# Second and fourth sums of the FFN up-projection weights formed by VectorE adds instead of accumulating DMAs; the first column group in the same order as the others

## The chip, the core and the metric

One NeuronCore of a Trainium2 chip runs the whole program. The metric is device microseconds from the program's start to its end, the median of several executions. The engines have a queue each and work them off in order: TensorE (PE, with its weight loads shown as PEld), VectorE (DVE), ScalarE (ACT), GpSimd (POOL) and SyncE (SP). Here SP issues the plain loads, and POOL issues the loads that add what they bring to what is already in the tile (accumulating DMAs).

## The reference

Two layers of a hybrid decoder trunk on 512 tokens of 1024 features, all float32. Each layer is a mixer with four branches, which the change does not touch, and a feed-forward network (FFN), which it does:

```python
    hf = rmsnorm(x, norm_ffn)
    gate, up = jnp.split(hf @ ffn_w_up, 2, axis=-1)
    return x + (jax.nn.silu(gate) * up) @ ffn_w_down
```

`ffn_w_up` is 1024 x 5632: the first 2816 columns are the gate's, the last 2816 the up half.

## The kernel before

Every float32 operand is split into a high and a low part, and a product is three matmuls (`mm3`): high by high, high by low, low by high. ScalarE makes the high part of a block of weights (`w_hi`), VectorE subtracts it from the raw block for the low part (`w_lo`).

The up-projection is done by the seven products of Strassen's scheme in Winograd's form instead of eight. The columns are taken in six groups (q from 0 to 5) of 512 of the gate's and 512 of the up half's; the last group has 256 of each. The rows (features) are parted into even and odd blocks of 128 and the tokens into two halves. With G0, G1 for the gate's even and odd rows of a group and U0, U1 for the up half's, the products read these blocks of weights (1 MB each):

- p1 reads G0 (in the code `B11` for q = 0), and writes the PSUM pair A
- p5 reads X = G0 + U0, the first sum, and writes C
- p6 reads X + U1, the second sum, and writes B
- p3 reads Y = U1, added to C
- p2 reads G1, added to A
- p7 reads Y + U0, the third sum, added to B
- p4 reads X + U1 + G1, the fourth sum, added to B

(The signs are in the features' sums, the tiles `s_hi` and `s_lo`, which are formed at the end of the mixer, and in the negative of the norm's factor, `nrstd_t`.) Each product is two parts, one per half of its block's rows (h0, h1, 512 KB each), and each part is 12 matmuls on 512 columns. Between products VectorE adds the PSUM pairs to scratch tiles (their names in the profile are `merged`), ScalarE and VectorE form silu times up, PE transposes the result (`turn`), and after groups 2 and 5 the down-projection follows (`down`).

All four sums of weights are formed before by accumulating DMAs: `Block.add` (line 1114) has POOL issue two DMAs with `accum_op=OP.add`. p5 issues those of the second sum at its end, p6 those of the fourth, p3 those of the third, and `first_sum` those of the first. The raw tile w_raw has two buffers, used in turn, and the tile f_raw, which belongs to the FFN alone, two more: X of groups 1 to 5 lies in f_raw, as does p2's block in group 0; all else lies in w_raw. Split blocks have three buffers, so a split can run at most three parts ahead of PE.

The first group has an order of its own, p1, p5, p2, p3, p6, p5 of the next group, p7, p4. All others run p1, p6, p3, p2, p7, p5 of the next group, p4. The order on each engine is set by the scheduler of the framework from the program's order and priorities; splits and additions of PSUM pairs are issued with a high priority. What it makes of the change is shown further down.

Of the kernel before, what the change touches and what calls it, by code (L numbers as in the profile page):

```python
# [17 lines left out]
OP = mybir.AluOpType  # L18
# [5 lines left out]
NT = S // P  # L24
# [19 lines left out]
AHEAD = 3000  # L44
# [25 lines left out]
def hybrid_trunk(ctx: ExitStack, tc: tile.TileContext, x, mem, positions, norm_mix, w_in, conv_w,  # L70
# [155 lines left out]
    def small(n, name="small", bufs=12):  # L226
        return consts.tile([P, 8], F32, name=name, bufs=bufs)[:, :n]
# [94 lines left out]
    def norm_token(ssq):  # L322
        ps = tr_ps()
        for t in range(NT):
            pe.matmul(ps[:, t:t + 1], ssq[:, t * P:(t + 1) * P], ones_d[:, 0:1], start=True, stop=True)
        r = small(NT, name="rstd_t", bufs=2)
        rstd_into(r, ps[:, :NT], small, NT)
        return r
# [772 lines left out]
    class Block:  # L1101
# [12 lines left out]
        def add(self, src, odd):  # L1114
            for i in range(2):
                nc.gpsimd.dma_start(self.raw[:, 2 * i:2 * i + 2, :], self.rows(src, odd, i), accum_op=OP.add)  # L1116
            return self

        def split(self):
            parts = []  # L1120
            for i in range(2):
                hi, lo = (wpool.tile([P, 1024], F32R, name=nm, bufs=W_BUFS)[:, :2 * self.n].rearrange("p (k n) -> p k n", n=self.n)
                          for nm in ("w_hi", "w_lo"))
                with tc.high_priority(offset=AHEAD):
                    A(hi, self.raw[:, 2 * i:2 * i + 2, :], AF.Copy)
                    dve.tensor_sub(lo, self.raw[:, 2 * i:2 * i + 2, :], f(hi))  # L1126
                parts.append((hi, lo))
            return parts

    def ffn(l, h, sx, ssq, xr, spare):  # L1130
# [9 lines left out]
        with tc.tile_pool(name="ffn", bufs=1) as fp:  # L1140
# [3 lines left out]
            def block(n, name="w_raw"):  # L1144
                if name == "w_raw":
                    t = wpool.tile([P, 2048], F32, name="w_raw", bufs=RAW_BUFS)
                else:
                    t = fp.tile([P, 2048], F32, name=name, bufs=2)
                return Block(t[:, :4 * n].rearrange("p (k n) -> p k n", n=n), n)

            def gate_w(q):
                return up[:, q * 512:q * 512 + widths[q]]

            def up_w(q):
                return up[:, FF + q * 512:FF + q * 512 + widths[q]]

            def product(pss, form, parts, first, mid=None):
                src, odd, s0 = form
                n = parts[0][0].shape[2]
                for i, (hi, lo) in enumerate(parts):  # L1160
                    for t in range(2):
                        for k in range(2):
                            kk = 2 * i + k
                            c = kk if odd is None else 2 * kk + odd
                            mm3(pss[t][:, :n], pair(src, c, slice(s0 + t * P, s0 + (t + 1) * P)),
                                (hi[:, k, :], lo[:, k, :]), first and kk == 0, kk == 3, not first)
                    if i == 0 and mid is not None:
                        mid()
# [16 lines left out]
            def accs(name):  # L1185
                return [bank[name]() for _ in range(2)]
# [10 lines left out]
            def p5(q):  # L1197
                d = st[q]
                d["C"] = accs("C")
                product(d["C"], S1, d["X"].split(), True)  # L1200
                d["X"].add(up_w(q), 1)

            def p1(q, mid=None):
                d = st[q]
                d["A"] = accs("A")
                w = d["B11"] if q == 0 else block(widths[q]).load(gate_w(q), 0)
                product(d["A"], A11, w.split(), True, mid)

            def silu_mul(dst, src, t, other):
                A(dst, src, AF.Silu, scale=norm["r"][:, t:t + 1])  # L1210
# [9 lines left out]
            def hi_prio():  # L1220
                return tc.high_priority(offset=AHEAD)
# [13 lines left out]
                residual(lambda m: xr[:, m, :], wd, a, kt, 256, h2, ssq2, lambda c: g_mix(l + 1, c), spill=end)  # L1235
                return h2, ssq2

            def p2(q):
                product(st[q]["A"], A12, block(widths[q], "w_raw" if q else "f_raw").load(gate_w(q), 1).split(), False)

            def p3(q):
                d = st[q]
                d["Y"] = block(widths[q]).load(up_w(q), 1)
                product(d["C"], S4, d["Y"].split(), False)
                d["Y"].add(up_w(q), 0)

            def p4(q):
                product(st[q]["B"], A22, st[q]["X"].split(), False)

            def p6(q):  # L1250
                d = st[q]
                d["B"] = accs("B")
                product(d["B"], S2, d["X"].split(), True)
                d["X"].add(gate_w(q), 1)

            def p7(q):
                product(st[q]["B"], S3, st[q]["Y"].split(), False)

            def plus(dst, src, ps, n):
                with hi_prio():  # L1260
                    for t in range(2):
                        dve.tensor_add(dst[t], src[t], ps[t][:, :n])

            def ahead(q):
                if q < Q:
                    p5(q)

            first_sum(0)
            for q in range(Q):
                n = widths[q]  # L1270
                d1, e, u, g = (tmps(i, n) for i in range(4))
                p1(q, flush)
                d = st[q]
                if q == 0:
                    p5(0)
                with hi_prio():
                    for t in range(2):
                        A(d1[t], d["A"][t][:, :n], AF.Copy)
                plus(e, d1, d["C"], n)
                if q == 0:  # L1280
                    r = norm_token(ssq)
                    nr = small(NT, name="nrstd_t", bufs=2)
                    dve.tensor_scalar(nr, r, -1.0, None, op0=OP.mult)
                    norm.update(r=r, n=nr)
                    p2(q)
                    p3(q)
                    plus(u, d1, d["C"], n)
                    first_sum(q + 1)
                    p6(q)
                    plus(u, u, d["B"], n)  # L1290
                else:
                    p6(q)
                    plus(u, d1, d["B"], n)
                    p3(q)
                    if q + 1 < Q:
                        first_sum(q + 1)
                    plus(u, u, d["C"], n)
                    p2(q)
                for t in range(2):
                    silu_mul(g[t], d["A"][t][:, :n], t, u[t])  # L1300
                if q == 0:
                    p5(q + 1)
                    turn(g, 0, q)
                p7(q)
                plus(e, e, d["B"], n)
                if q:
                    turn(g, 0, q)
                    ahead(q + 1)
                p4(q)
                plus(d1, d1, d["B"], n)  # L1310
                for t in range(2):
                    silu_mul(d1[t], d1[t], t + 2, e[t])
                pending.append((d1, 2, q))
                if q in ends:
                    flush()
                    res = down(q)
# [40 lines left out]
```

## Time and profile before

| what | value |
|---|---|
| timed runs, median of 3 | 2050.01 us (2049.25 to 2051.16) |
| profiled execution, its own time | 2053.13 us |
| its span | 2051.4 us |
| mean granted clock of TensorE | 0.99 |
| FFN of layer 0, of layer 1 (first matmul of p1) | from 712.1 us, from 1697.9 us |
| moved by DMA | 250.01 MB, of which 46.28 MB by POOL's accumulating DMAs and its few others |

The profile's page gives busy time by engine, then the span in 40 slices, the queues, the chain of work that ended last, and the costliest groups. In its rows "L284 PE MATMUL B<-w_hi,s_hi" is line, engine, operation and the tiles it writes and reads; a bracket at the end holds the idle time of the engine just before the instruction and what ended it. Matmuls overlap, so the time between the starts of two of them is their cost. Times in the timeline are us from the span's start. "SPq" and "POOLq" are DMAs issued by SP and POOL, with the time from issue to landing.

### The profile page before, as it was taken

The numbers are of one execution on the slowest core, as the hardware profiler recorded it, in microseconds if no ns is written. First come the engines' busy times: TensorE is split into PE (matmuls) and PEld (weight loads), VectorE is DVE, ScalarE is ACT, GpSimd is POOL, SyncE is SP. The second block draws the span as 40 slices with busy tenths as digits, with TensorE's granted clock in tenths as the row PEclk, the third lists the DMA queues.
The fourth block names the chain that finished last, engine by engine and source line by source line (L and its number), as shares of the span: only waits on it lengthen the run. The fifth ranks groups of instructions, "written<-read, shape, count | busy, mean of one in ns | idle before, by whom it ended". The sixth has DMA issues, their size and how long they took to land.

```text
span 2051.4 us, 27620 instructions
## 1 busy us (share of the span) xinstructions
PE 2014.5 (98%) x10440; PEld 1699.4 (83%) x10440; DVE 1374.4 (67%) x2673; ACT 1112.9 (54%) x1978; POOL 126.5 (6%) x132
## 2 busy tenths in 40 slices
PE   7899999999999989999999999999999999999999
PEld 7898988888888868888889898878888887888887
DVE  5668899637766757537656899963677676663662
ACT  6554565866565535324445555577667655541541
POOL 1000000000000022102100000000000002210210
PEclk8999999999999999999999999999999999999999
DMA  6622122212214498738452222221222349782852
GB/s 219 231 94 88 57 93 93 93 62 83 83 62 151 120 222 194 176 113 185 104 184 74 93 77 93 93 93 42 82 74 81 128 119 228 188 209 99 174 128 92
DMA packets 190904, 250.01 MB, mean 122 GB/s; under 512 B 6690, under 2 KB 134772, under 8 KB 190644
## 3 DMA queue, kind: packets, MB, share of 16 engines
q1 hardware_dynamic: 160800, 193.55, 28.8%
q0 software_dynamic: 26368, 46.28, 13.3%
q10 hardware_dynamic: 3604, 8.43, 1.1%
q8 instruction: 82, 1.34, 0.3%
q14 instruction: 50, 0.41, 0.1%
HBM read 237.74 MB, written 10.49 MB: 121 GB/s over the span
## 4 chain that ended last, share of the span: by engine, by line
PE 90%; DMA 5%; issue 2%; DVE 1%; POOL 1%; ACT 1%; SPq 0%; POOLq 0%; ACTq 0%
PE mm L284 18%; PE mm L285 18%; PE mm L286 18%; PE B L284 4%; PE B L286 4%; PE B L285 4%; PE A L286 3%; PE A L285 3%; PE A L284 3%; DMA w_raw<-in_ffn_w_up_dram 2%; DMA f_raw<-in_ffn_w_up_dram 1%; PE C L285 1%; PE C L284 1%; PE C L286 1%; PE tr L734 1%
## 5 line engine op out<-in xcount | busy, mean ns | idle before, releaser
L119 ACT ACTIVATE w_hi<-w_raw 128x1024 fp32r<-128x1024 f32 (+1 forms) x362 | 373.2, 1032 | 440.6 <-PE mm L285 137.3
L249 DVE TENSOR_TENSOR w_lo<-w_raw,w_hi 128x1024 fp32r<-128x1024 f32 x258 | 311.9, 1210 | 223.0 <-ACT w_hi L119 219.6
L284 PE MATMUL mm<-h_hi,w_hi 128*128 128x512 f32 x960 | 378.7, 395 | 0.0
L285 PE MATMUL mm<-h_lo,w_hi 128*128 128x512 f32 x960 | 377.3, 393 | 0.0
L286 PE MATMUL mm<-h_hi,w_lo 128*128 128x512 f32 x960 | 375.3, 393 | 0.0
L286 PEld LDWEIGHTS mm<-h_hi,w_lo 128*128 128x128 f32 x960 | 180.4, 188 | 37.5 <-issue 0.7
L284 PEld LDWEIGHTS mm<-h_hi,w_hi 128*128 128x128 f32 x960 | 180.5, 188 | 37.3 <-issue 2.0
L285 PEld LDWEIGHTS mm<-h_lo,w_hi 128*128 128x128 f32 x960 | 180.5, 188 | 36.7 <-issue 1.7
L1126 DVE TENSOR_TENSOR w_lo<-w_raw,w_hi 128x1024 fp32r<-128x1024 f32 (+1 forms) x104 | 118.8, 1142 | 94.4 <-ACT w_hi L119 93.8
L286 PE MATMUL mm<-w_hi,h_lo 128*128 128x256 f32 (+1 forms) x448 | 127.9, 286 | 0.0
L284 PE MATMUL mm<-w_hi,h_hi 128*128 128x256 f32 (+1 forms) x448 | 127.1, 285 | 0.0
L285 PE MATMUL mm<-w_lo,h_hi 128*128 128x256 f32 (+1 forms) x448 | 126.9, 284 | 0.0
L284 PE MATMUL mm<-y_hi,w_hi 128*128 128x512 f32 x256 | 102.3, 401 | 0.0
L286 PE MATMUL mm<-y_hi,w_lo 128*128 128x512 f32 x256 | 101.5, 397 | 0.0
L285 PE MATMUL mm<-y_lo,w_hi 128*128 128x512 f32 x256 | 101.3, 396 | 0.0
L1116 POOL DMA_DIRECT2D f_raw<-in_ffn_w_up_dram x60 | 75.5, 1287 | 414.9 <-DVE w_lo L1126 337.7
L1126 DVE TENSOR_TENSOR w_lo<-f_raw,w_hi 128x1024 fp32r<-128x1024 f32 (+1 forms) x64 | 72.0, 1125 | 39.7 <-ACT w_hi L119 39.4
L119 ACT ACTIVATE w_hi<-f_raw 128x1024 fp32r<-128x1024 f32 (+1 forms) x64 | 62.7, 980 | 63.4 <-PE B L286 33.0
L286 PEld LDWEIGHTS mm<-w_hi,h_lo 128*128 128x128 f32 x448 | 85.6, 191 | 1.4 <-issue 0.8
L284 PEld LDWEIGHTS mm<-w_hi,h_hi 128*128 128x128 f32 x448 | 85.2, 191 | 1.2 <-issue 0.8
L285 PEld LDWEIGHTS mm<-w_lo,h_hi 128*128 128x128 f32 x448 | 85.4, 191 | 0.6
L1116 POOL DMA_DIRECT2D w_raw<-in_ffn_w_up_dram x36 | 48.0, 1435 | 550.8 <-DVE xc L1076 245.0
(422 smaller groups left out, 4605.7 us busy)
## 6 DMA issues: line engine op xcount, KB each, us to landing
w_raw<-in_w_in_dram SPq DMA_DIRECT2D x72, 1024.0 KB, 5.0
w_raw<-in_ffn_w_up_dram SPq DMA_DIRECT2D x60, 512.0 KB, 4.5
f_raw<-in_ffn_w_up_dram POOLq DMA_DIRECT2D x48, 512.0 KB, 7.5
w_raw<-in_ffn_w_down_dram SPq DMA_DIRECT2D x18, 1024.0 KB, 5.3
w_raw<-in_w_lift_dram SPq DMA_DIRECT2D x32, 512.0 KB, 3.4
w_raw<-in_ffn_w_up_dram POOLq DMA_DIRECT2D x32, 512.0 KB, 7.4
f_raw<-in_ffn_w_up_dram SPq DMA_DIRECT2D x20, 512.0 KB, 4.9
w_raw<-in_mem_w_kv_dram SPq DMA_DIRECT2D x8, 1024.0 KB, 6.8
```

Source lines behind the costliest of these rows:

```text
L119: i = act.activation(dst, src, func, **kw)
L249: dve.tensor_sub(lo, raw[:, k:e], f(hi))
L284: pe.matmul(ps, ah, bh, start=first, stop=False, skip_group_check=go_on)
L285: pe.matmul(ps, ah, bl, start=False, stop=False, skip_group_check=go_on)
L286: pe.matmul(ps, al, bh, start=False, stop=last, skip_group_check=go_on)
L734: pe.matmul(pv[e * HD:(e + 1) * HD, :], vt[:, b, :], pt[:, b, e * 2 * P:(e + 1) * 2 * P], start=b == 0, stop=b == t)
L1116: nc.gpsimd.dma_start(self.raw[:, 2 * i:2 * i + 2, :], self.rows(src, odd, i), accum_op=OP.add)
L1126: dve.tensor_sub(lo, self.raw[:, 2 * i:2 * i + 2, :], f(hi))
```

## The change

`Block.plus` is new: it adds another raw block to this one with two VectorE operations of 128 x 1024 elements, one per half. Y and G1, which are loaded for p3 and p2 anyway, are what it adds: p6 now loads Y first and adds it to X, and p2 adds its own block to X after its split. The accumulating DMAs at the end of p5 and of p6 are gone; those of the first and the third sum stay. The special order of the first group is gone too: all six run p1, p6, p3, p2, p7, p5 of the next, p4, where p5 of group 0 follows its p1. What is computed is the same.

```diff
+        def plus(self, other):
+            for i in range(2):
+                with tc.high_priority(offset=AHEAD):
+                    k = slice(2 * i, 2 * i + 2)
+                    dve.tensor_add(self.raw[:, k, :], self.raw[:, k, :], other.raw[:, k, :])
...
                 product(d["C"], S1, d["X"].split(), True)
-                d["X"].add(up_w(q), 1)
...
             def p6(q):
                 d = st[q]
                 d["B"] = accs("B")
+                d["Y"] = block(widths[q]).load(up_w(q), 1)
+                d["X"].plus(d["Y"])
                 product(d["B"], S2, d["X"].split(), True)
-                d["X"].add(gate_w(q), 1)
...
             def p3(q):
                 d = st[q]
-                d["Y"] = block(widths[q]).load(up_w(q), 1)
                 product(d["C"], S4, d["Y"].split(), False)
                 d["Y"].add(up_w(q), 0)
...
             def p2(q):
-                product(st[q]["A"], A12, block(widths[q], "w_raw" if q else "f_raw").load(gate_w(q), 1).split(), False)
+                d = st[q]
+                w = block(widths[q], "w_raw" if q else "f_raw").load(gate_w(q), 1)
+                product(d["A"], A12, w.split(), False)
+                d["X"].plus(w)
...
                 if q == 0:
                     p5(0)
+                    r = norm_token(ssq)
+                    nr = small(NT, name="nrstd_t", bufs=2)
+                    dve.tensor_scalar(nr, r, -1.0, None, op0=OP.mult)
+                    norm.update(r=r, n=nr)
...
-                if q == 0:
-                    r = norm_token(ssq)
...
-                    p2(q)
-                    p3(q)
-                    plus(u, d1, d["C"], n)
-                    first_sum(q + 1)
-                    p6(q)
-                    plus(u, u, d["B"], n)
-                else:
-                    p6(q)
-                    plus(u, d1, d["B"], n)
-                    p3(q)
-                    if q + 1 < Q:
-                        first_sum(q + 1)
-                    plus(u, u, d["C"], n)
-                    p2(q)
+                p6(q)
+                plus(u, d1, d["B"], n)
+                p3(q)
+                if q + 1 < Q:
+                    first_sum(q + 1)
+                plus(u, u, d["C"], n)
+                p2(q)
```

Since lines move, w_lo of the FFN's blocks is line 1126 before and 1132 after, and the new adds are line 1123.

How the engines' orders change is shown at three places. The first is the start of layer 0's first group, on VectorE. Before, from the split of X's first half (the first row) to the last piece of the features' sums (`s_lo`), with h_lo the low part of the last two blocks of features, and the semaphores that each row waits for:

```order
L1126 TENSOR_TENSOR w_lo<-w_raw,w_hi 128x1024 [waits DMASW0_49,Activation_49]
L307 TENSOR_TENSOR ssq<-ssq,sq 128x512 [waits Activation_49]
L1048 TENSOR_TENSOR gate<-gate 128x256 [waits DVE_49,Activation_49]
L1053 TENSOR_TENSOR h_lo<-gate,h_hi 128x512 [waits Activation_49]
L1049 SCALAR_TENSOR_TENSOR gate<-gate 128x256 [waits DVE_49]
L1053 TENSOR_TENSOR h_lo<-gate,h_hi 128x512 [waits Activation_49]
L1050 SCALAR_TENSOR_TENSOR gate<-gate 128x256 [waits DVE_49]
L1126 TENSOR_TENSOR w_lo<-w_raw,w_hi 128x1024 [waits DMASW1_49,Activation_49]
L1056 TENSOR_TENSOR s_lo<-gate,s_hi 128x512 [waits Activation_49]
L1056 TENSOR_TENSOR s_lo<-gate,s_hi 128x256 [waits Activation_49]
```

And the same stretch of the change:

```order
L1132 TENSOR_TENSOR w_lo<-w_raw,w_hi 128x1024 [waits DMASW0_49,Activation_49]
L307 TENSOR_TENSOR ssq<-ssq,sq 128x512 [waits Activation_49]
L1048 TENSOR_TENSOR gate<-gate 128x256 [waits DVE_49,Activation_49]
L1123 TENSOR_TENSOR w_raw<-w_raw 128x1024 [waits DMAHW7_49,DVE_49]
L1053 TENSOR_TENSOR h_lo<-gate,h_hi 128x512 [waits Activation_49]
L1049 SCALAR_TENSOR_TENSOR gate<-gate 128x256 [waits DVE_49]
L1053 TENSOR_TENSOR h_lo<-gate,h_hi 128x512 [waits Activation_49]
L1132 TENSOR_TENSOR w_lo<-w_raw,w_hi 128x1024 [waits DMASW1_49,Activation_49]
L1050 SCALAR_TENSOR_TENSOR gate<-gate 128x256 [waits DVE_49]
L1056 TENSOR_TENSOR s_lo<-gate,s_hi 128x512 [waits Activation_49]
L1123 TENSOR_TENSOR w_raw<-w_raw 128x1024 [waits DMAHW0_49,DVE_49]
L1132 TENSOR_TENSOR w_lo<-w_raw,w_hi 128x1024 [waits Activation_49]
```

The two adds of Y to X (DMAHW7 and DMAHW0 are the loads of Y's halves) now stand between, the first ahead of both h_lo; the last row is already w_lo of p6's first half, and s_lo's last piece comes behind it.

The second place is the same time on ScalarE, in the change: from the split of X's second half to the blocks of p3 (w_hi from w_raw) and p2 (w_hi from f_raw). The rows with `small` and the table load are the norm's factor, `merged<-A` the copies of p1's result.

```order
L119 ACTIVATE w_hi<-w_raw 128x1024 [waits PE_49]
L119 ACTIVATE s_hi<-gate 128x256 [waits DVE_49]
L119 ACTIVATE small<-tr,eps 128x4 [waits PE_49]
L119 ACTIVATE merged<-A 128x512 [waits PE_49]
L119 ACTIVATE small<-small,half 128x4 [waits Activation_49]
L115 ACT_TABLE_LOAD
L119 ACTIVATE merged<-A 128x512 [waits PE_49]
L119 ACTIVATE w_hi<-w_raw 128x1024 [waits DVE_49]
L119 ACTIVATE small<-small 128x4 [waits Activation_49]
L119 ACTIVATE w_hi<-w_raw 128x1024 [waits DMAHW7_49,PE_49]
```

Before, the first of these rows was not there and p2's first block, from f_raw, stood ahead of the norm's rows. Now the first row is w_hi of p6's first half, and w_hi of its second half (the row that waits for DVE) stands behind the norm, the table load and both copies.

The third place is VectorE in the third group of layer 0, p6 and p3. Before:

```order
L1126 TENSOR_TENSOR w_lo<-f_raw,w_hi 128x1024 [waits DMASW2_49,Activation_49]
L1211 SCALAR_TENSOR_TENSOR merged<-merged,nrstd_t 128x512 [waits Activation_49] x2
L1126 TENSOR_TENSOR w_lo<-f_raw,w_hi 128x1024 [waits DMASW3_49,DVE_49,Activation_49]
L1126 TENSOR_TENSOR w_lo<-w_raw,w_hi 128x1024 [waits DMAHW7_49,DVE_49,Activation_49]
L1262 TENSOR_TENSOR merged<-merged,C 128x512 [waits Activation_49]
```

And in the change:

```order
L1132 TENSOR_TENSOR w_lo<-f_raw,w_hi 128x1024 [waits Activation_49]
L1240 SCALAR_TENSOR_TENSOR merged<-merged,nrstd_t 128x512 [waits Activation_49] x2
L1123 TENSOR_TENSOR f_raw<-f_raw,w_raw 128x1024 [waits DMAHW3_49,DVE_49]
L1132 TENSOR_TENSOR w_lo<-f_raw,w_hi 128x1024 [waits Activation_49]
L1123 TENSOR_TENSOR f_raw<-f_raw,w_raw 128x1024 [waits DMAHW4_49,DVE_49]
L1132 TENSOR_TENSOR w_lo<-w_raw,w_hi 128x1024 [waits Activation_49]
L1270 TENSOR_TENSOR merged<-merged,C 128x512 [waits Activation_49]
```

The w_lo rows from f_raw are p6's two halves, that from w_raw p3's first. The adds of G1 (DMAHW3 and DMAHW4 are the loads of its halves) stand between them, so that w_lo of p6's second half comes behind a wait for the load of p2's block. The second sum's adds stand further up, about one product earlier.

On POOL the accumulating DMAs of an FFN fall from 48 to 24. In the first group X of the next group (f_raw) still stands ahead of Y (w_raw). The order of SP's loads stays, but for p2's block of group 0, which now comes behind X of group 1.

More of the change, by code (lines that the diff above doesn't have):

```diff
@@ L1207, in p1, with p6, p3, p2 @@
                 product(d["A"], A11, w.split(), True, mid)
+            def p6(q):
+                d = st[q]
+                d["B"] = accs("B")
+                d["Y"] = block(widths[q]).load(up_w(q), 1)
+                d["X"].plus(d["Y"])
+                product(d["B"], S2, d["X"].split(), True)
+            def p3(q):
+                d = st[q]
+                product(d["C"], S4, d["Y"].split(), False)
+                d["Y"].add(up_w(q), 0)
+            def p2(q):
+                d = st[q]
+                w = block(widths[q], "w_raw" if q else "f_raw").load(gate_w(q), 1)
+                product(d["A"], A12, w.split(), False)
+                d["X"].plus(w)
+            def p7(q):
+                product(st[q]["B"], S3, st[q]["Y"].split(), False)
+            def p4(q):
+                product(st[q]["B"], A22, st[q]["X"].split(), False)
             def silu_mul(dst, src, t, other):
@@ L1236, in down @@
                 return h2, ssq2
-            def p2(q):
-                product(st[q]["A"], A12, block(widths[q], "w_raw" if q else "f_raw").load(gate_w(q), 1).split(), False)
-            def p3(q):
-                d = st[q]
-                d["Y"] = block(widths[q]).load(up_w(q), 1)
[L1244 to L1253, printed above, removed]
-                d["X"].add(gate_w(q), 1)
-            def p7(q):
-                product(st[q]["B"], S3, st[q]["Y"].split(), False)
             def plus(dst, src, ps, n):
@@ L1262, in plus @@
                         dve.tensor_add(dst[t], src[t], ps[t][:, :n])
-            def ahead(q):
-                if q < Q:
-                    p5(q)
             first_sum(0)
@@ L1279, in ffn @@
                 plus(e, d1, d["C"], n)
-                if q == 0:
-                    r = norm_token(ssq)
-                    nr = small(NT, name="nrstd_t", bufs=2)
-                    dve.tensor_scalar(nr, r, -1.0, None, op0=OP.mult)
-                    norm.update(r=r, n=nr)
-                    p2(q)
-                    p3(q)
-                    plus(u, d1, d["C"], n)
-                    first_sum(q + 1)
-                    p6(q)
-                    plus(u, u, d["B"], n)
-                else:
-                    p6(q)
-                    plus(u, d1, d["B"], n)
-                    p3(q)
-                    if q + 1 < Q:
-                        first_sum(q + 1)
-                    plus(u, u, d["C"], n)
-                    p2(q)
+                p6(q)
+                plus(u, d1, d["B"], n)
+                p3(q)
+                if q + 1 < Q:
+                    first_sum(q + 1)
+                plus(u, u, d["C"], n)
+                p2(q)
                 for t in range(2):
                     silu_mul(g[t], d["A"][t][:, :n], t, u[t])
-                if q == 0:
-                    p5(q + 1)
-                    turn(g, 0, q)
                 p7(q)
                 plus(e, e, d["B"], n)
-                if q:
-                    turn(g, 0, q)
-                    ahead(q + 1)
+                turn(g, 0, q)
+                if q + 1 < Q:
+                    p5(q + 1)
                 p4(q)
```

## The prediction

> **What bounds the kernel now.** I read the page first, for the engine that is always busy.
>
> ```profile
> span 2051.4 us, 27620 instructions
> PE 2014.5 (98%) x10440; PEld 1699.4 (83%) x10440; DVE 1374.4 (67%) x2673; ACT 1112.9 (54%) x1978; POOL 126.5 (6%) x132
> ```
>
> TensorE is the bound. The change removes no matmul, so it can only win back time in which PE stands or runs at half rate, and it can only lose by making PE stand. So the next view is the table by stretches: each layer's FFN cut into its first group and the rest (columns: PE, PEld, DVE, ACT and POOL busy, granted clock, DMA share, GB/s).
>
> ```profile
> 712.00:772.00 60.00, 52.13 (x223) 42.28 (x223) 34.88 (x46) 27.49 (x35) 14.49 (x12) 0.91 0.90 212
> 772.00:1072.00 300.00, 299.87 (x1441) 252.00 (x1440) 175.37 (x217) 127.19 (x162) 41.30 (x37) 1.00 0.63 158
> 1698.00:1750.00 52.00, 47.97 (x208) 38.94 (x207) 30.54 (x40) 24.63 (x33) 14.53 (x12) 0.93 1.01 238
> 1750.00:2051.00 301.00, 297.23 (x1428) 249.46 (x1426) 165.02 (x200) 114.98 (x142) 40.61 (x34) 1.00 0.60 147
> ```
>
> Groups two to six leave nothing to win: PE is busy 299.87 of 300 us. Everything to win lies in the two first groups, where the clock is down too. The timeline of PE gives the pieces; the first two rows are a product undisturbed: 24 matmuls in 5.44 us, 0.227 us each.
>
> ```profile
> 1715.75 0.62 PE L284 MATMUL C<-w_hi,s_hi 128*128 128x512 f32 x2
> 1721.19 0.62 PE L284 MATMUL B<-w_hi,s_hi 128*128 128x512 f32 x2
> ...
> 723.72 0.28 PE L325 MATMUL tr<-ones_d,ssq 128*128 128x1 f32 x2
> 725.24 0.73 PE L284 MATMUL A<-w_hi,h_hi 128*128 128x512 f32 x2 [1.25 <-ACT w_hi L119]
> 726.50 0.50 PE L285 MATMUL A<-w_lo,h_hi 128*128 128x512 f32 x1 [0.53 <-DVE w_lo L1126]
> 727.54 0.59 PE L286 MATMUL A<-w_hi,h_lo 128*128 128x512 f32 x1
> 731.41 0.40 PE L285 MATMUL A<-w_lo,h_hi 128*128 128x512 f32 x1
> ...
> 762.16 0.76 PE L284 MATMUL B<-w_hi,h_hi 128*128 128x512 f32 x1 [6.09 <-DVE merged L1262]
> 765.21 0.39 PE L285 MATMUL B<-w_lo,h_hi 128*128 128x512 f32 x1
> ...
> 1742.46 0.76 PE L284 MATMUL B<-w_hi,h_hi 128*128 128x512 f32 x1 [3.89 <-DVE merged L1262]
> 1748.14 0.41 PE L285 MATMUL B<-w_lo,h_hi 128*128 128x512 f32 x1
> ```
>
> Layer 0, first wait (p2's weights): 1.25 + 0.53, then 10 matmuls from 727.54 to 731.41, 3.87 us where 2.27 would do: 1.60 lost at half rate. Second wait (p4, the fourth sum): 6.09, then 7 matmuls in 3.05 us: 1.46 lost. Layer 1, at p4 only: 3.89, then 13 matmuls in 5.68 us: 2.73 lost. In all 10.9 + 6.6 = **17.5 us, the most that the change can win**.
>
> What ended the waits at p4 stands on ScalarE, which makes w_hi, and in the DMA view of the jam:
>
> ```profile
> 755.06 1.06 ACT L119 ACTIVATE w_hi<-w_raw 128x1024 fp32r<-128x1024 f32 x1 [6.95 <-DMA w_raw<-in_ffn_w_up_dram]
> 759.10 2.00 ACT L119 ACTIVATE w_hi<-w_raw 128x1024 fp32r<-128x1024 f32 x2 [2.01 <-DMA w_raw<-in_ffn_w_up_dram]
> ...
> q0 software_dynamic: 1666, 3.20, 102.8%
> w_raw<-in_ffn_w_up_dram POOLq DMA_DIRECT2D x2, 512.0 KB, 15.8
> ```
>
> From 740 to 757 us the engines did little but POOL's accumulating transfers: 3.20 MB in 17 us, **2.8 us for one of 512 KB**; p4's two took 15.8 us to land.
>
> **The change part by part.** *Removed*: four of eight accumulating transfers a group, 48 in all (40 of 512 KB, 8 of 256), 4 x 2.8 = 11 us of DMA time a group, with POOL's issues. POOL is off the path; the worth is that p4's sum waits no more for the queue, and that p2 no longer comes before its weights. So all 17.5 us go, and the sum is about what is late next.
>
> *Added*: 48 VectorE adds. The trace has none; the nearest row is an operation of the same shape that also reads two SBUF operands.
>
> ```profile
> L1126 DVE TENSOR_TENSOR w_lo<-f_raw,w_hi 128x1024 fp32r<-128x1024 f32 x52 | 63.7, 1225 | 36.1 <-ACT w_hi L119 36.0
> ```
>
> 1.23 us (1.14 back to back); 40 such and 8 of half the width make about 54 us. In the four stretches above VectorE is busy 405.8 of 713 us; it would be 460, 65%. The adds hide under PE unless one stands in VectorE's order ahead of a w_lo that PE is about to need. Between nothing and 54 us I take what these orders give, place by place.
>
> *First group, layer 0.* The adds wait for Y (w_raw, free once B11 is split):
>
> ```profile
> 711.58 0.88 SPq L1111 DMA_DIRECT2D w_raw<-in_ffn_w_up_dram  x2
> w_raw<-in_ffn_w_up_dram SPq DMA_DIRECT2D x2, 512.0 KB, 4.6
> ...
> 714.94 0.42 DVE L1048 TENSOR_TENSOR gate<-gate 128x256 f32<-128x256 f32 x1
> 720.48 1.09 ACT L119 ACTIVATE merged<-A 128x512 f32<-128x512 f32 x2 [2.67 <-PE A L286]
> 725.10 0.25 ACT L119 ACTIVATE small<-tr,eps 128x4 f32<-128x4 f32 x1
> 725.38 0.30 ACT L119 ACTIVATE small<-small,half 128x4 f32<-128x4 f32 x1
> 725.69 1.28 ACT L115 ACT_TABLE_LOAD   x1
> ```
>
> Y lands at 716.2; VectorE is at the add from 715.4, waits 0.8 and adds for 1.2. So all behind it, h_lo first, comes 2 us later, which is still ahead of PE: its last matmuls of p1 and p5 need these pieces between 720 and 723.5 (723.72 before, with the norm's matmuls). Free. Then ScalarE. w_hi of p6's first half gets its buffer when the last matmul on B11 is done, about 721.2 in the new order of PE, and takes 1.06; s_hi's last piece takes 0.4: 722.7. Ahead of w_hi of the second half now stand two small operations of the norm, both copies of A (0.55 each) and the table load: 0.25 + 0.55 + 0.30 + 1.28 + 0.55 gives 725.7, and w_hi is there at 726.8. PE, which starts p6 at 723.5, needs it after 12 matmuls, at 726.2: 0.6 wait. The w_hi of p3's first half follows at 727.9, and after two matmuls PE's order has two of p3: 0.7 more. At p2 two adds and two accumulations stand ahead of its w_lo in VectorE's order: 0.9. At p7 Y's transfers stand behind X(1)'s in POOL's order. X(1)'s load goes out when the last s_lo is done, 724.1 now, and lands 4.6 later, 728.7; from there the third transfer of four needs 3 x 2.8 and some 2 to land (a load of 4.5 us moves for about half of them): 739 alone, 741 beside X(2)'s load. With w_hi and w_lo PE could go on at 743; it asks at 723.5 + 3 x 5.44 + 2.2 of waits = 742: 1.0. That makes 3.2; with half of the 1.6 that short waits cost at 727.54, I take **4** (1.5 to 9).
>
> *First group, layer 1.* Here the table load stands behind both w_hi of p6 in ScalarE's order, and PE reaches p6 where it reached p2 before, at 1715.75 - 5.44 = 1710.3. In the same replay every part is ready before PE asks, the nearest by 0.5 us. I take **0.5** (0 to 4).
>
> *Groups two to six.* VectorE's order is now: w_lo of p6's first half, add of the gate's first half, w_lo of p6's second half, second add. The add waits for a plain load that goes out when p1's block is split, about as PE starts p1. If that load is slow, w_lo is late though its own data are there. The third group of layer 0 before:
>
> ```profile
> 808.88 0.94 SPq L1111 DMA_DIRECT2D w_raw<-in_ffn_w_up_dram  x2
> f_raw<-in_ffn_w_up_dram POOLq DMA_DIRECT2D x2, 512.0 KB, 8.1
> w_raw<-in_ffn_w_up_dram SPq DMA_DIRECT2D x2, 512.0 KB, 7.3
> ...
> 813.12 1.23 DVE L1126 TENSOR_TENSOR w_lo<-f_raw,w_hi 128x1024 fp32r<-128x1024 f32 x1 [0.22 <-ACT w_hi L119]
> 814.50 0.62 PE L284 MATMUL B<-w_hi,s_hi 128*128 128x512 f32 x2
> 820.81 1.22 DVE L1126 TENSOR_TENSOR w_lo<-w_raw,w_hi 128x1024 fp32r<-128x1024 f32 x1
> 823.58 0.61 PE L284 MATMUL C<-w_hi,s_hi 128*128 128x512 f32 x2
> ```
>
> The load takes 7.3 us beside the next X's first sum: 816.2. Add until 817.4, w_lo until 818.6 (813.12 + 1.23 before), where PE, p6 begun at 814.50 and 8 transposes later, asks at 818.4; second add, p3's first w_lo until 820.8, five short operations of 0.6, p3's second w_lo 823.8 to 825.0, asked for at 824.0. Some 0.2 + 0.9. The fifth group's load takes 7.1 us, and in layer 1 the orders are alike: 4 x 0.9 = **3.6** (0 to 12). In the other groups the load has no such company; with the middle value of all of them the halves are there by p6's start: nothing.
>
> ```profile
> w_raw<-in_ffn_w_up_dram SPq DMA_DIRECT2D x2, 512.0 KB, 7.1
> w_raw<-in_ffn_w_up_dram SPq DMA_DIRECT2D x25, 512.0 KB, 4.5
> ```
>
> Sum: 17.5 - 4 - 0.5 - 3.6 = 9.4 us won. The profiled execution took 2053.13 us (2051.4 and 1.7 around it) and would take 2043.7; it lies 3.1 above the median of the three timed runs, 2050.01, so the forecast for these is 2050.0 - 9.4 = **2040.6**.
>
> A rule on the clock: at 727.54 half rate followed waits of only 1.25 and 0.53 us. The Trainium skill (TensorE: Matmul & The Clock Gate, Part 1) says the clock is halved after about 3.4 us of idleness in a free-running window and released after as long a busy one. By it the short new waits would cost only themselves, and the time would be 2039.8; the row says more. The two long gaps agree with it.
>
> **The rivals.** (a) *Nothing is late.* A little slack in each of these orders and all 17.5 us are won: 2032.5. For it: most of my waits are under 1 us, at the limit of such a replay. Against it: the load of 7.3 us is measured.
>
> (b) *Short waits keep the clock down.* If each of the seven new waits costs 1.6 at half rate as at 727.54, 11.2 less 0.8 counted go: 2051.0, no change. Against it, in the row below, a wait of 0.43 in layer 1, after which the clock stayed at 1.00.
>
> ```profile
> 1697.50 0.63 PE L1037 MATMUL tr<-ident,xc 128*128 128x128 f32 x4 [0.43 <-ACT w_hi L119]
> 1700.00:1702.00 2.00, 2.00 (x10) 1.67 (x9) 2.00 (x5) 1.95 (x5) 0.31 (x1) 1.00 0.51 81
> ```
>
> (c) *The queue still jams at p7.* X(1)'s and Y's transfers, X(2)'s load and the delayed f_raw loads meet; Y lands at 745 and PE loses 3.2 and 2.7 at half rate in layer 0: 0.8 was counted, so 2045.7. For it: p4's transfers took 15.8 us in such company. Against it: half of that company is gone.
>
> (d) *VectorE stands at loads: slower.* In groups two to six of both layers the add of the gate's first half holds back w_lo. It decides at 818.4 - 2 x 1.23 = 815.9, a landing 7.0 us after the issue; at 10 PE stands 3 us in each of ten groups, and with 2.7 at half rate (as at 1742.46) it is 57 us less 17.5: 2089. For it: 7.3 and 7.1 are at the point already. Against it: with half the accumulating bytes gone loads can hardly take longer than before.
>
> (e) *The sums stay late.* If the adds ran but p4's gap had another cause, only the 3.4 us of p2 would come back and my new waits would stay: 2050.0 - 3.4 + 8.1 = 2054.7. The rows at 755.06 and 759.10 speak against it.
>
> **How the numbers follow.** The forecast's own spread, 2036 to 2045, has 0.48; (a) 0.15; (c) 0.14; (b) 0.12; (d) 0.08; (e) 0.03. The range has to take in (a), (c) and (b): 2032 to 2052. A measurement of this kernel tells about 0.2%, 4.1 us, from no change, so faster is below 2045.9: the forecast, (a) and over half of (c), 0.71; no change 0.19; slower (d), (e) and the upper edge of (b), 0.10.
>
> **What would show it.** In the profile after: no wait of PE over 1.5 us in either first group and a granted clock of 0.97 or more there; in layer 0 short waits at p6's second half, ended by ScalarE's w_hi, and at p7, ended by w_raw's transfer; 48 adds of 1.2 us, those of the gate's first half in the third and fifth groups idle before a DMA; software transfers down from 46.28 MB by 23.1. I am wrong if PE still waits over 3 us in a first group, if the adds' idle time before DMAs shows in groups two, four and six too, or if a wait under 1 us pulls the clock down.

## The result and the profile after

| | before | after |
|---|---|---|
| median of 6 runs | 2050.93 us (2049.25 to 2052.93) | 2039.45 us (2038.21 to 2040.99) |
| profiled execution, span | 2053.13 us, 2051.4 us | 2039.99 us, 2038.3 us |
| TensorE busy | 98% | 99% |
| VectorE busy | 67% | 70% |
| software transfers | 46.28 MB | 23.21 MB |

The ratio is 0.9944 (0.9932 to 0.9957): 11.5 us faster, 8.8 to 13.9 with the interval. Forecast were 9.4 us, 2040.6. Run again beside the last experiments, the changed kernel came to 0.9955 (0.9942 to 0.9967), 9.2 us, a little outside the 0.001 around 0.9944 that I had expected of it. The intervals of the two overlap, and the forecast lies between them.

The page of after, its engines and the queue of the accumulating transfers:

```profile
PE 2011.1 (99%) x10440; PEld 1695.1 (83%) x10440; DVE 1418.7 (70%) x2721; ACT 1112.4 (55%) x1978; POOL 68.9 (3%) x84
q0 software_dynamic: 13312, 23.21, 7.0%
```

48 instructions more on VectorE, with 44 us more busy time where 54 had been estimated; 48 fewer on POOL; 23.07 MB less on the software queue, as forecast. The first three stretches of before (the third moved to where layer 1's first group now stands, and 60 us long instead of 52; columns PE, PEld, DVE, ACT and POOL busy, granted clock, DMA share, GB/s):

```profile
712.00:772.00 60.00, 58.47 (x266) 47.34 (x265) 48.55 (x61) 32.33 (x43) 9.60 (x8) 1.00 0.67 179
772.00:1072.00 300.00, 299.47 (x1444) 251.03 (x1443) 187.99 (x235) 127.21 (x166) 17.90 (x18) 1.00 0.48 132
1690.00:1750.00 60.00, 59.22 (x271) 48.33 (x270) 48.68 (x61) 32.57 (x42) 9.59 (x8) 1.00 0.71 176
```

In both first groups PE is busy but for 1.5 and 0.8 us of 60, and the clock is at 1.00, where it was 0.91 and 0.93. Where the time came from is read off two marks in PE's timeline, p1's first matmul in layer 0 and in layer 1. Before, then after:

```profile
712.07 0.39 PE L284 MATMUL A<-w_hi,h_hi 128*128 128x512 f32 x1
1697.88 0.48 PE L284 MATMUL A<-w_hi,h_hi 128*128 128x512 f32 x1
```

```profile
711.22 0.39 PE L284 MATMUL A<-w_hi,h_hi 128*128 128x512 f32 x1
1689.10 0.48 PE L284 MATMUL A<-w_hi,h_hi 128*128 128x512 f32 x1
```

Of the 13.1 us between the two spans, 0.85 lie ahead of layer 0's FFN, where nothing was changed: chance. From mark to mark 7.9 us are gained (layer 0's FFN; 5.1 forecast: 10.9 less 4 less half of 3.6), and from the second mark to the end 4.3 (layer 1's; 4.3 forecast).

### The profile page after: what moved, and what is told of

It reads as the page before. It is cut to its first block, busy times and chain, and to the rows that moved or that the text cites. A ratio compares the mean times of both kernels' runs of the same rounds, so it can differ in the third digit from the quotient of the medians.

```text
span 2038.3 us, 27510 instructions
## 1 busy us (share of the span) xinstructions
PE 2011.1 (99%) x10440; PEld 1695.1 (83%) x10440; DVE 1418.7 (70%) x2721; ACT 1112.4 (55%) x1978; POOL 68.9 (3%) x84
## 3 DMA queue, kind: packets, MB, share of 16 engines
q0 software_dynamic: 13312, 23.21, 7.0%
## 4 chain that ended last, share of the span: by engine, by line
PE 94%; DMA 3%; DVE 1%; ACT 1%; issue 0%; POOL 0%; SPq 0%; ACTq 0%; DVEq 0%; POOLq 0%
PE mm L284 19%; PE mm L285 18%; PE mm L286 18%; PE B L285 4%; PE B L286 4%; PE B L284 4%; PE A L286 4%; PE A L284 4%; PE A L285 4%; PE C L285 2%; PE C L284 2%; PE C L286 2%; DMA w_raw<-in_ffn_w_up_dram 1%; PE tr L734 1%; PE tr L728 1%; PE at L705 1%
## 5 line engine op out<-in xcount | busy, mean ns | idle before, releaser
L119 ACT ACTIVATE prob<-prob,small 128x128 f32<-128x128 f32 (+3 forms) x128 | 69.2, 554 | 15.4 <-DVE small L717 14.8
L285 PE MATMUL B<-w_lo,s_hi 128*128 128x512 f32 (+1 forms) x192 | 71.7, 375 | 1.1 <-DVE w_lo L1132 1.1
```

The source lines that it names most:

```text
L119: i = act.activation(dst, src, func, **kw)
L285: pe.matmul(ps, ah, bl, start=False, stop=False, skip_group_check=go_on)
```

## What is late now

The product p7 of layer 0's first group, on PE and then on ScalarE:

```profile
739.80 0.73 PE L284 MATMUL B<-w_hi,s_hi 128*128 128x512 f32 x2 [0.26 <-ACT w_hi L119]
741.06 0.50 PE L285 MATMUL B<-w_lo,s_hi 128*128 128x512 f32 x1 [0.53 <-DVE w_lo L1132]
741.40 0.39 PE L286 MATMUL B<-w_hi,s_lo 128*128 128x512 f32 x1
...
743.84 0.73 PE L284 MATMUL B<-w_hi,s_hi 128*128 128x512 f32 x2 [0.21 <-ACT w_hi L119]
745.10 0.50 PE L285 MATMUL B<-w_lo,s_hi 128*128 128x512 f32 x1 [0.53 <-DVE w_lo L1132]
```

```profile
718.24 1.06 ACT L119 ACTIVATE w_hi<-w_raw 128x1024 fp32r<-128x1024 f32 x1 [0.98 <-PE C L286]
...
723.36 1.05 ACT L119 ACTIVATE w_hi<-w_raw 128x1024 fp32r<-128x1024 f32 x1
...
738.69 1.06 ACT L119 ACTIVATE w_hi<-w_raw 128x1024 fp32r<-128x1024 f32 x1 [6.21 <-DMA w_raw<-in_ffn_w_up_dram]
742.73 1.06 ACT L119 ACTIVATE w_hi<-w_raw 128x1024 fp32r<-128x1024 f32 x1 [2.98 <-DMA w_raw<-in_ffn_w_up_dram]
```

1.5 us of short waits, all at p7 and all behind Y's accumulating transfers, which land at 738.7 and 742.7. PE goes on at 0.23 us a matmul right behind each wait, so the clock did not drop. The wait forecast at p6 is not there: its two w_hi start at 718.24 and 723.36.

The largest wait left in groups two to six stands in layer 1's third group. VectorE, and then PE:

```profile
1782.20 1.23 DVE L1123 TENSOR_TENSOR f_raw<-f_raw,w_raw 128x1024 f32<-128x1024 f32 x1 [2.15 <-DMA w_raw<-in_ffn_w_up_dram]
1783.35 1.22 DVE L1132 TENSOR_TENSOR w_lo<-f_raw,w_hi 128x1024 fp32r<-128x1024 f32 x1
1786.19 1.22 DVE L1123 TENSOR_TENSOR f_raw<-f_raw,w_raw 128x1024 f32<-128x1024 f32 x1 [1.63 <-DMA w_raw<-in_ffn_w_up_dram]
1787.33 1.22 DVE L1132 TENSOR_TENSOR w_lo<-w_raw,w_hi 128x1024 fp32r<-128x1024 f32 x1
1788.47 0.68 DVE L1270 TENSOR_TENSOR merged<-merged,C 128x512 f32<-128x512 f32 x1
1789.20 0.50 PE L284 MATMUL C<-w_hi,s_hi 128*128 128x512 f32 x1 [1.06 <-DVE merged L1270]
```

VectorE stands at both adds of G1, p2's block (2.15 and 1.63 us), and what comes too late behind the second is the addition that reads p5's result out of the bank C, to which p3 wants to add. In the profile of the second measurement the same place cost 3.4 us, at w_lo and at that addition:

```profile
1785.93 1.23 DVE L1123 TENSOR_TENSOR f_raw<-f_raw,w_raw 128x1024 f32<-128x1024 f32 x1 [4.84 <-DMA w_raw<-in_ffn_w_up_dram]
1788.34 0.50 PE L285 MATMUL B<-w_lo,s_hi 128*128 128x512 f32 x1 [1.44 <-DVE w_lo L1132]
1792.88 0.50 PE L284 MATMUL C<-w_hi,s_hi 128*128 128x512 f32 x1 [1.95 <-DVE merged L1270]
```

All waits of PE inside the two FFNs come to 4.0 us in the first profile of after and 6.7 in the second: the difference lies in the third and fifth groups, at such loads (1.3 us and 4.6).

## The experiments

The ratio is that of the medians to those of before in the same rounds; "us" is that ratio taken of 2051. "PE waits" are all waits of PE inside the two FFNs of the profiled execution, without the time at half rate behind them. With each edit the scheduler orders the engines anew, so that a run can differ from its neighbour at more places than the edit; where that is seen to matter, it is said.

| kernel | ratio (95%) | us against before | PE waits, us | half rate |
|---|---|---|---|---|
| before | 1 | | 12.2 | 3 times |
| order only | 0.9994 (0.9985 to 1.0002) | -1 | 11.1 | twice |
| sums only | 0.9969 (0.9958 to 0.9980) | -6 | 9.0 | once |
| second sum only | 0.9978 (0.9969 to 0.9987) | -5 | 8.9 | once |
| fourth sum only | 0.9992 (0.9983 to 1.0001) | -2 | 9.6 | once |
| after, first and second measurement | 0.9944 and 0.9955 | -11 and -9 | 4.0 and 6.7 | never |
| after, late additions | 0.9927 (0.9913 to 0.9940) | -15 | 1.4 | never |
| after, Y first on POOL | 0.9938 (0.9925 to 0.9952) | -13 | 5.3 | never |
| after, both edits | 0.9920 (0.9907 to 0.9934) | -16 | 1.5 | never |
| after, additions twice | 0.9986 (0.9977 to 0.9996) | -3 | 8.9 | once |
| both edits, additions twice | 0.9967 (0.9955 to 0.9978) | -7 | 6.9 | never |

**Order only**: the kernel before, with the first group's calls in the order of the change and all sums still by transfers.

```diff
                 if q == 0:
-                    p2(q)
-                    p3(q)
-                    plus(u, d1, d["C"], n)
-                    first_sum(q + 1)
-                    p6(q)
-                    plus(u, u, d["B"], n)
-                else:
-                    p6(q)
...
+                p6(q)
+                plus(u, d1, d["B"], n)
+                p3(q)
+                if q + 1 < Q:
+                    first_sum(q + 1)
```

> The kernel before with one part of the change: the first group in the common order, all four sums still accumulating transfers. Theory PLACE (the gain sits in two waits; what decides is whose transfers stand ahead on POOL's queue): the wait at p2 (3.4 us) goes, the fourth sum's two transfers now stand ahead of X(1)'s and Y's, so the wait at p4 goes too but turns up at p7: 7 to 11 us in layer 0 and 2 to 5 in layer 1 (after had 1.5 and 0). Time 2045 to 2052. Rival ORDER (the order alone carries the gain): within 2 us of 2039.5. Rival SUMS (the additions alone carry it): as before, 2051, with p4's waits of 6.1 and 3.9 in place.

The time is as PLACE had it (SUMS had the same time, but with p4's waits in place), the places only in part. p2's and p4's waits are gone. In layer 0 p6 waits 1.6 us and p7 4.1, less than the 7 to 11 forecast; in layer 1 it is not p7 that waits but p6, 4.6 us. Each long wait drew the clock down behind it. The order by itself is worth nothing that can be told from zero.

**Sums only**: the changed kernel, with the first group's calls in the old order.

```diff
             def p3(q):
+                if q == 0:
+                    d["Y"] = block(widths[q]).load(up_w(q), 1)
+                    d["X"].plus(d["Y"])
                 product(d["C"], S4, d["Y"].split(), False)
...
                 product(d["B"], S2, d["X"].split(), True)
+                if q == 0:
+                    d["X"].plus(d["W"])
```

> The changed kernel with the first group back in the order of before (Y loaded and added to X ahead of p3, the gate's block added behind p6). PLACE: p2's wait of 1.2 + 0.5 us and its half-rate stretch of 1.6 in layer 0 stay, p4's waits of 6.1 and 3.9 are gone, p7 has none. Time 2039 to 2043. ORDER: 2049 to 2051. SUMS: 2039.5. For the clock: if waits of 1.2 + 0.5 us pull it down again at this place, PE takes 3.5 us or more for the ten matmuls behind them; if not, 2.3.

2044.6 on the scale of before at 2051, 1.6 above PLACE's range, and neither rival's. p4's waits are 0.4 in both layers, p7 has none. In layer 0 p2 waits longer than before, since the load of its block lands at 726.3 instead of 724.1:

```profile
727.43 0.73 PE L284 MATMUL A<-w_hi,h_hi 128*128 128x512 f32 x2 [3.11 <-ACT w_hi L119]
728.69 0.80 PE L285 MATMUL A<-w_lo,h_hi 128*128 128x512 f32 x1 [0.53 <-DVE w_lo L1132]
729.28 0.63 PE L286 MATMUL A<-w_hi,h_lo 128*128 128x512 f32 x1
```

The clock was down behind it, so that the seven matmuls from 728.69 on took 3.0 us. With a wait of this length the run does not answer what waits of 1.2 and 0.5 us do to the clock at this place. The third groups' waits of 1.7 and 1.9 us, which I had left out of the range, make up the rest. So both halves of the change are needed: each leaves one of the two first-group waits in place or moves it.

**Second sum only**: `d["X"].plus(w)` in p2 is taken out and p6 ends with an accumulating transfer.

```diff
                 product(d["B"], S2, d["X"].split(), True)
+                d["X"].add(gate_w(q), 1)
...
-                d["X"].plus(w)
```

> The changed kernel with the fourth sum an accumulating transfer again: 24 additions instead of 48. PLACE: its two transfers (2.8 us each) stand ahead of Y's on POOL's queue in the first groups, so p7 waits about 5.6 us more in layer 0 and 2 in layer 1, with 1.5 to 2.7 us at half rate behind each: 2046 to 2051. The wait of 1.1 us in layer 1's third group is gone. Rival BYTES (the gain goes with the accumulating bytes taken away, wherever): half of the 11.5 us, 2045.

The time does not part the two theories: 2046.5 of 2051 is at the lower edge of PLACE's range, and its interval of 2044.6 to 2048.3 takes in the 2045 of BYTES. In the trace PLACE holds. p7 of layer 0:

```profile
744.22 0.73 PE L284 MATMUL B<-w_hi,s_hi 128*128 128x512 f32 x2 [1.07 <-ACT w_hi L119]
745.48 0.50 PE L285 MATMUL B<-w_lo,s_hi 128*128 128x512 f32 x1 [0.52 <-DVE w_lo L1132]
...
751.32 0.73 PE L284 MATMUL B<-w_hi,s_hi 128*128 128x512 f32 x2 [3.28 <-ACT w_hi L119]
752.58 0.80 PE L285 MATMUL B<-w_lo,s_hi 128*128 128x512 f32 x1 [0.53 <-DVE w_lo L1132]
```

5.4 us where after had 1.5, so 3.9 more and not 5.6, with half rate behind the last; 1.2 us at p7 in layer 1 too, where after had none; and the waits in the third groups that end with the addition of C are gone.

**Fourth sum only**: X's second sum is an accumulating transfer again, at the end of p5.

```diff
                 product(d["C"], S1, d["X"].split(), True)
+                d["X"].add(up_w(q), 1)
...
-                d["X"].plus(d["Y"])
```

> The changed kernel with the second sum an accumulating transfer again: 24 additions. PLACE: its transfers go out while POOL's queue is empty, land before p6 asks but for 0 to 3 us in layer 0, and leave the queue free for X(1) and Y: 2039 to 2043, most of the gain. BYTES: 2045.

Both theories missed: 2049.4, hardly a gain. Layer 0 does as PLACE said (1.7 us at p6). Layer 1 loses what was won there; POOL, then PE:

```profile
1702.10 1.20 POOL L1116 DMA_DIRECT2D f_raw<-in_ffn_w_up_dram  x1 [8.43 <-DMA f_raw<-in_ffn_w_up_dram]
1702.83 1.69 POOL L1116 DMA_DIRECT2D w_raw<-in_ffn_w_up_dram  x1
1711.62 1.22 PE L284 MATMUL B<-w_hi,s_hi 128*128 128x512 f32 x2 [5.06 <-ACT w_hi L119]
1712.64 1.15 PE L284 MATMUL C<-w_hi,s_hi 128*128 128x512 f32 x2
```

In POOL's order X(1)'s first transfer (f_raw) stands ahead of the second half of X's second sum (w_raw), and POOL waits for the load of X(1) before it issues either: VectorE had done with X's half at 1700.9, its transfer goes out at 1702.83, behind one of X(1) and ahead of another, and lands at 1710.5, 7.7 us later. p6 stands for 5.06 us and goes on at half rate. The same three issues stand in the same order where the first experiment lost 4.6 us. So PLACE seems to need an addition: on POOL not only the transfers ahead in the queue count, but what POOL itself waits for. Here that was 1.9 us until the issue; no run puts the three issues in another order, so what each part is worth is argued and not shown. BYTES falls: its 2045 lies outside this run's interval, 2047.5 to 2051.2.

**Late additions**: a dependency puts the fourth sum's two additions on VectorE behind the addition of C to u.

```diff
-                d["X"].plus(w)
+                d["X"].plus(w, d["behind"])
...
-                plus(u, u, d["C"], n)
+                d["behind"] = plus(u, u, d["C"], n)
```

> The changed kernel with the fourth sum's two additions ordered on VectorE behind the addition of C to u (after p3), where the gate's block has landed in every group. If VectorE standing at these loads is what makes PE wait in layer 1's third and fifth groups (1.1 and 0.3 us, ended by VectorE's addition of a product), these waits go and the additions' idle time before transfers of w_raw falls from 24.4 us to a few: 0 to 2 us faster than the changed kernel. Rival: the gate's raw buffer is held longer, the next group's loads go out later, and PE waits for a w_hi at p1 or p6 instead: 1 us or more slower, with new waits in groups two to six.

More than expected: 5.1 us faster than the changed kernel in the same rounds (2038.20 against 2043.27), because in these rounds there was more to win: its waits are 1.4 us against 6.7. The third and fifth groups of both layers have none left over 0.2, and the rival's new waits did not come. The other half of the expectation failed: VectorE still stands idle for 19.6 us ahead of additions until a load of w_raw has landed, where a few were expected (24.4 in the first profile of after, 30.7 in the second). PE does not notice: nothing that it needs soon stands behind them.

**Y first on POOL**: X(1)'s two transfers are ordered behind Y's.

```diff
-                st[q]["X"].load(gate_w(q), 0).add(up_w(q), 0)
+                st[q]["X"].load(gate_w(q), 0).add(up_w(q), 0, st[0]["Y"] if q == 1 else None)
```

> The changed kernel with one edit on POOL: X(1)'s two accumulating transfers are issued behind Y's two in both first groups. If Y's place behind X(1)'s (2 x 2.8 us) is what makes PE wait at p7 in layer 0 (0.3 + 0.5 + 0.2 + 0.5 us), these waits go, w_hi of p7's first half stands ready some 4 us before PE asks, and the time falls by 1 to 1.5 us. Rival: X(1) is now the late one and PE waits at p5 of the second group instead, in layer 0 or 1: no gain or a loss of some us.

PE has no wait at all in layer 0's first group. Behind Y, X(1) was in time; the time fell by 2 us, which the intervals of two such kernels do not separate, so the trace carries this.

**Both edits**:

> The two edits together. If both mechanisms hold, the sum: 1 to 3.5 us faster than the changed kernel and no wait of PE over 0.7 us left in either FFN. If one of the rivals holds, no better than the better of the two.

7.1 us faster than the changed kernel in the same rounds (2036.13 against 2043.27), twice the most that was expected and the best of all, with one wait over 0.7 us left (0.8, at a w_hi of layer 0's down-projection). POOL issues Y's two transfers at 726.61 and 728.04 and X(1)'s behind them. ScalarE in layer 0's first group:

```profile
733.58 1.06 ACT L119 ACTIVATE w_hi<-w_raw 128x1024 fp32r<-128x1024 f32 x1 [1.66 <-PE C L286]
736.30 1.06 ACT L119 ACTIVATE w_hi<-w_raw 128x1024 fp32r<-128x1024 f32 x1 [1.66 <-PE A L286]
```

Both of p7's w_hi wait for a buffer that PE gives back, and no longer for Y, 5.1 and 6.4 us earlier than at 738.69 and 742.73.

**Additions twice**, in the changed kernel and in the one with both edits:

```diff
                     dve.tensor_add(self.raw[:, k, :], self.raw[:, k, :], other.raw[:, k, :])
+                    dve.tensor_add(self.raw[:, k, :], self.raw[:, k, :], other.raw[:, k, :])
```

> The changed kernel with each of the 48 additions done twice (its sums are not the reference's): VectorE gets 54 us more, all inside the FFNs. Theory COVER (an addition costs nothing unless it stands ahead of what PE needs next): the time rises only by what the places with no slack lose, up to 1.14 us at each: the first group's p6 and p7 in layer 0 and the third and fifth groups: 3 to 10 us, with PE's waits in the trace adding up to the rise. Rival WORK (VectorE is near enough to the bound that its time counts): 27 to 54 us slower. Half rate behind a wait only where PE stands for over 2.5 us in all.

> The version with both edits (late additions, Y ahead of X(1) on POOL) with each addition done twice, so that its sums are not the reference's either. COVER: with the fourth sum out of the way of the other operations less of the 54 us shows: 0 to 4 us slower than that version, 2036 to 2041 on the scale of before at 2052. WORK: 27 to 54 us slower than it, as much as the other doubled run.

```profile
PE 2014.6 (98%) x10440; PEld 1697.0 (83%) x10440; DVE 1467.8 (72%) x2769; ACT 1111.7 (54%) x1978; POOL 68.9 (3%) x84
```

VectorE was busy 49 us more. The changed kernel became 6 to 9 us slower (0.9986 against 0.9955 and 0.9944), inside COVER's range and far from WORK's. But that range was met in part by luck. 6.1 us stand at one place in layer 0, a wait of 3.15 and 2.9 lost at half rate behind it, and VectorE's time is not what makes it:

```profile
740.50 1.22 PE L284 MATMUL B<-w_hi,s_hi 128*128 128x512 f32 x2 [3.15 <-ACT w_hi L119]
741.52 0.63 PE L285 MATMUL A<-w_lo,h_hi 128*128 128x512 f32 x1
```

In this kernel's order two matmuls of p7 (into B) stand in the middle of p2 (into A); in after they stand behind it. So PE asks for p7's w_hi earlier, while Y's transfer lands at 739.4 instead of 738.7. The same place cost 1.5 us in after, so 4.5 of the 6 to 9 us go with it. The version with both edits lost 9.6 us, where 0 to 4 were expected: COVER's number failed there. Its waits are many and short (0.2 to 1.3 us, 6.9 in all against 1.5), and none lies in a first group: about 2.5 us at a w_lo, 2.0 behind ScalarE's splits and copies, 2.2 in the down-projections, where a split waits for the load of its weights. They make up about half of the loss; the other half stays unexplained. An eighth to a fifth of the 49 us comes out as time, order changes included; the rest lies under PE.

## Why the prediction came out

- **The cap.** 17.5 us in the first groups' waits and the half rate behind them. Right: the waits at p2 and p4 are gone, and so are all stretches at half rate; the kernel with both edits wins 16 of the 17.5. A wait of 0.55 us near the end of layer 1 (at 1985.0 before, at a w_hi) had been left out of it. That the waits at p4 came from the queue of accumulating transfers is borne out by the kernel with only the sums changed: 0.4 us left in each layer.
- **Layer 0's first group, 4 us.** The sum was too large and one step was wrong. "w_hi of p6's first half gets its buffer when the last matmul on B11 is done" failed: it started at 718.24, released by a matmul on C (p5), and not at 721.2. That is 3.0 us before the time given, of which 0.85 us is the earlier start of the whole FFN. So w_hi of p6's second half was not pushed behind its need by the table load, and the 1.3 us were 0. p2's 0.9 was 0 too. p7 was right in cause and near in size: 1.5 measured, 1.0 forecast, and the edit on POOL took it away. The 0.8 for a lower clock was 0.
- **Layer 1's first group, 0.5 us.** 0.6, at p3's w_lo; in the second profile nothing.
- **Groups two to six, 3.6 us.** The mechanism is right and shown: with the additions moved behind p3, these waits go. The size was too small for the second profile (4.6 us) and too large for the first (1.3), since it hangs on how long the load beside an accumulating transfer takes. In layer 0's third group of the first profile it took 5.8 us instead of 7.3, and the second w_lo of p3 was needed later than forecast:

```profile
799.09 0.95 SPq L1111 DMA_DIRECT2D w_raw<-in_ffn_w_up_dram  x2
804.91 1.23 DVE L1123 TENSOR_TENSOR f_raw<-f_raw,w_raw 128x1024 f32<-128x1024 f32 x1 [1.81 <-DMA w_raw<-in_ffn_w_up_dram]
...
813.24 1.22 DVE L1132 TENSOR_TENSOR w_lo<-w_raw,w_hi 128x1024 fp32r<-128x1024 f32 x1
```

```profile
813.86 0.62 PE L284 MATMUL C<-w_hi,s_hi 128*128 128x512 f32 x2
814.32 0.62 PE L284 MATMUL A<-w_hi,h_hi 128*128 128x512 f32 x2
814.77 0.39 PE L285 MATMUL C<-w_lo,s_hi 128*128 128x512 f32 x1
```

  Four matmuls that need only w_hi stand in PE's order ahead of the first that needs w_lo; I had counted two. What I had not seen at all is that the addition which empties a PSUM bank stands behind the same waits.
- **The sum.** The mechanisms hold, but that the total came so near is partly luck: the first term was 2.5 us too large, and the third moves by 3 us between two executions. A wait of 0.5 us at a w_lo of layer 0's down-projection, in both profiles of after and not before, was not in the sum.
- **The signs.** No wait over 1.5 us in a first group and a clock of 1.00 there came true, as did VectorE's idle time ahead of G1's additions in the third and fifth groups; the wait at p6 did not. One sign of being wrong did show: VectorE stands idle ahead of additions, until a load lands, in groups two, four and six as well (1.0, 3.6 and 1.1 us in layer 0, for the first of Y's). PE did not wait there. So idle time of VectorE was the wrong sign to look for; a late w_lo, or a late addition out of PSUM, is the right one.
- **The additions at nothing.** Right within limits: with all of them doubled the kernels became 6 to 10 us slower, not 54, and part of that is a new order.
- **The rivals.** (a) fell: something is late in each profile. (b) fell: none of the new waits lowered the clock, and no wait under 2.3 us did so inside the FFNs in any profile but that of before. (c) is what happens when two more transfers stand ahead of Y, as in the kernel with the second sum only; in after the queue is short enough. (d) was seen in mild form: in layer 1's third group the addition could start 6.2 us after the load's issue in the first profile, and 8.9 in the second. The second is past the 7.0 that I had put as the point, and w_lo was late by 1.4 us; in the other groups no w_lo was. (e) fell with the waits at p4.

## What to carry to other kernels

When a queue that executes in order makes a product wait, list everything that it has to issue ahead of that product's piece, waits included: with a quarter of the queue's transfers taken away a wait of 5 us was there, in the kernel with the fourth sum only, and one swap in the queue's order took away p7's 1.5 us. Work that is moved to an engine with time to spare costs little as work and something as a wait, or by the new order that the scheduler makes of it: put an operation that waits for a load behind what other engines need next, close to its own use. After an edit whose gain lies in two waits, try each half alone: here the halves were worth 1 and 6 us and the whole 9 to 11.

## What the runs showed of the hardware

**It is not the length of a wait alone that lowers the clock, but how little PE does in one step of 3.41 us.** In the kernel with the fourth sum only there are two waits of about the same length as p2's before:

```profile
727.80 0.73 PE L284 MATMUL B<-w_hi,s_hi 128*128 128x512 f32 x2 [1.19 <-ACT w_hi L119]
729.06 0.50 PE L285 MATMUL B<-w_lo,s_hi 128*128 128x512 f32 x1 [0.53 <-DVE w_lo L1132]
```

From here matmuls follow each other by 0.23 us, full rate, though the waits are 1.19 and 0.53; before, 1.25 and 0.53 were followed by 1.6 us lost. The same pair (1.07 or 1.08 and 0.52 or 0.53) left the clock up in the kernels with the order only and the second sum only; so did 1.44 and 1.95 us with 2.6 us of work between in the second profile of after, and one of 2.28 in the kernel with Y first. Waits of 3.1 us and more were followed by half rate each time (3.11, 3.15, 3.28, 3.89, 4.12, 4.61, 5.06, 6.09).

The granted clock tells more. In each kept trace the times between two of its changes are whole multiples of 3.41 us, and each half-rate stretch inside the FFNs lasts 3.41 or 6.83 us. Cut into such steps of 3.41 us, before and the kernel with the fourth sum only look like this (columns as above; the clock stands third from the end):

```profile
724.17:727.58 3.41, 1.81 (x7) 1.20 (x8) 1.73 (x2) 2.75 (x4) 0.00 (x0) 1.00 1.07 314
727.58:730.99 3.41, 3.41 (x10) 2.64 (x9) 2.16 (x2) 2.79 (x4) 1.35 (x2) 0.50 0.59 228
```

```profile
723.71:727.12 3.41, 2.89 (x13) 2.06 (x12) 0.00 (x0) 0.43 (x1) 1.18 (x1) 1.00 1.07 295
727.12:730.53 3.41, 2.21 (x8) 1.53 (x9) 2.76 (x4) 3.35 (x6) 1.19 (x1) 1.00 1.09 336
```

Before, both waits fall into one step, in which PE runs 7 matmuls of the 15 that fit, and the clock is down from its end. In the other kernel a step ends inside the first of them: 13 matmuls run in the one and 8 in the next, and the clock stays up. So p2's case of before need not be an exception; whether waits of a microsecond or two cost half rate hangs on where the steps fall, and they fall differently in each kept trace. How much work in a step is enough these profiles do not tell (7 matmuls left the clock up once, in the kernel with Y first), and no run moved one kernel against the steps. The Trainium skill (TensorE: Matmul & The Clock Gate, Part 1) gives a free-running window of about 3.4 us; the 3.41 us here agree with it. Here a window need not be idle throughout: before, the clock fell after steps in which PE was busy for 1.81 us and, at p4 of layer 0, for 1.18.

**A plain load beside an accumulating transfer is not a steady cost.** The 6.2 and 8.9 us named with rival (d) are the same load in two executions of the same kernel, from SyncE's issue (these rows, of the first and of the second) to the addition shown above:

```profile
1776.03 1.97 SPq L1111 DMA_DIRECT2D w_raw<-in_ffn_w_up_dram  x2
```

```profile
1777.06 1.88 SPq L1111 DMA_DIRECT2D w_raw<-in_ffn_w_up_dram  x2
```

A single profile therefore says how a wait comes about, but not how long it is on average.
